# DeepNorm layer: last tile's norm sums on TensorE at the fifth K step, one normalised tile more in the first FFN block, FFN sums issued behind a later weight's split

## The chip, the cores and the metric

One core of a Trainium2 chip runs the whole kernel. The metric is the device time of one execution in microseconds. Several executions of the kernel before were timed, and one more was profiled; shares and durations come from that one.

## The reference, cut to what matters

One layer of a decoder with 256 tokens and 16 meta tokens in front (T = 272), width D = 2048, FFN width 5632, all in float32. Attention and pooling are finished where the change begins. What bears on it:

```
mix = concat(A, B) @ W_o ;  h = LN(alpha*h + mix)
z = h @ w_up                       # 2 x 5632 columns
z = causal conv of width 3 over tokens, + bias
a, g = split(z) ;  f = (gelu(a) * g) @ w_down
h = LN(alpha*h + f)
```

Both layer norms take mean and variance over the 2048 channels of a token.

## The kernel before, in words

**Tiles.** Channels lie on the 128 partitions, so h is KT = 16 tiles of 128 channels by NQ = 258 tokens (two tokens of lead for the convolution). A weight tile is 128 x 2048 float32. TensorE works on float32 in two parts: ScalarE rounds a tile to an upper part (L127, 1024 columns at a time) and VectorE subtracts it to get the lower part (L128). A product of two such tiles is three matmuls (L199 to L201). Sixteen K steps of three make one block.

**Weights.** `stream` lists all weight tiles in the order of use; `weights()` takes the next and has the tiles up to two ahead fetched and split (`prefetch`, `emit`, `fetch`), with three raw and three split buffers. A transfer starts on SP's queue when VectorE has finished with the raw buffer. `split[i]` keeps the last upper and lower instruction of tile i. `tc.issue_after(x)` makes the scheduler place what is inside behind instruction x on its engine; `behind(i)` does so for both parts of tile i. The scheduler orders each engine's queue at build time, and each engine then works in order.

**First norm.** `output(m)` makes tile m of `W_o`'s product and adds it to the residual y (L628). `about_k(m)` subtracts a rough mean (L645), squares (ScalarE, L647), and GpSimd adds tile and square into the running sums s1 and s2 (L649 to L653). It also makes `folded[m]`, tile m times the norm's scale in two parts (L656 to L660): the first blocks of the FFN start on these before the norm is known. `deviation()` sums s1 and s2 over partitions with a matmul against ones (`sum_rows`, L246, true float32), turns them with VectorE (L251), works out mean and deviation (L685 to L690, the power on GpSimd, L689) and spreads them over the rows `rs` and `m2` (L255).

**First FFN blocks.** For f < FOLDED = 4, two halves each, the block's product runs on `folded`, and `unfold` (L727 to L732) applies `rs` and `m2` afterwards. In the first of these eight blocks `deviation()` is called after K step 8. Behind each of the eight, `normalise(m)` makes normalised tiles `h_parts` (L700 and L701 on VectorE, L702 and L704 on ScalarE, L705 on VectorE): two per block. The ninth block needs all sixteen.

**FFN plan.** `ffn_plan()` interleaves one up block with one down weight of the part before. A down part is multiplied with seven products for eight (Strassen's scheme): weights of kind "A" have four products (P2, P3, P1, P5), those of kind "B" three (P7, P6, P4), each three matmuls of 512 columns (L784 to L786). Kinds A and B need subtractions on the raw weight first (L118; L122 to L124). After the last weight of a kind the products are added to the result y2: at an A end `add(c11, P2)` and `add(c12, P3)` on VectorE (L792), with copies of P1 and P5 on ScalarE (L796, L798) and accumulating transfers on GpSimd's queue (L801, L802); at a B end `add(c22, v)`, L806, L807, `add(c21, P4)`, and three transfers (L809 to L811). PSUM has four buffers for these products.

**Turning the residual.** In the blocks b = 0 to 3 behind the folded ones, VectorE turns y's 16 tiles (L855), so many per block as a tuple says; from b = 4 on `residual` moves them with transfers on ScalarE's queue (L712).

Of the kernel before, what the change touches and what calls it, by code (L numbers as in the profile page):

```python
# [14 lines left out]
ALU = mybir.AluOpType  # L15
AX = mybir.AxisListType

P = 128
# [5 lines left out]
NQ = T - Q0  # L24
KT = D // P
# [13 lines left out]
NE = NQ + 2  # L39
ALPHA = 2.0 ** 0.25  # L40
# [5 lines left out]
W = (T + 31) // 32 * 32  # L46
# [22 lines left out]
def tile_layer(ctx, tc, xt, w_first, w_proj, w_uk, w_uv, w_pool, w_o, w_up, w_down, cols, rows, rel_bias, onehot, out):  # L69
    nc = tc.nc  # L70
# [16 lines left out]
    ps = small()  # L87
# [8 lines left out]
    for item in plan:  # L96
        if item[0] == "up":
            stream.append(w_up[item[2] * FT + item[1]])
        elif item[0] == "down":
            n = PARTS[FAST]  # L100
# [5 lines left out]
    spare, last = len(stream) - PARTS[-1], len(stream) - 1  # L106
    ready, raws, split = {}, {}, {}
    state = {"next": 0, "use": 0}
# [84 lines left out]
    def product(ps, hl, m, act, lo, hi, ks=range(KT), width=P, k0=0, k1=KT):  # L193

        for n in range(k0, k1):
            k = ks[n]
            wh, wl = hl[:, 0, k * width:k * width + m], hl[:, 1, k * width:k * width + m]
            ah, al = act[k][:, 0, lo:hi], act[k][:, 1, lo:hi]
            nc.tensor.matmul(ps, wh, ah, start=n == 0, stop=False)  # L199
            nc.tensor.matmul(ps, wh, al, start=False, stop=False)  # L200
            nc.tensor.matmul(ps, wl, ah, start=False, stop=n == KT - 1)  # L201
# [6 lines left out]
    for k0, k1 in [(k, k + 1) for k in range(9)] + [(9, 12), (12, 15), (15, 16)]:  # L208
# [6 lines left out]
        if k0 % 6 == 0:  # L215
            hl = wp.tile([P, 2, 2048 + 2], F32R, tag="whl", name="whl")
# [17 lines left out]
    ones = sb.tile([P, P], F32, name="ones")  # L234
# [7 lines left out]
    def sum_rows(s):  # L242

        ps = small()
        for n, t in enumerate(s):
            nc.tensor.matmul(ps[:, :W], ones, t, start=n == 0, stop=n == len(s) - 1)  # L246
        return ps[:, :W]

    def to_partitions(r, row):

        nc.vector.transpose(r, row)  # L251
# [19 lines left out]
    ps = heads[0][0]  # L271
# [22 lines left out]
    for j in range(2):  # L294
        ps = heads[1 + j][0]
        nc.scalar.activation(ct[:, j, :], ps[:, :T], AF.Copy)
        sq = temp([P, W], "sq")
# [4 lines left out]
    ps = small()  # L302
# [66 lines left out]
    for j in range(8):  # L369
        hl = weights()  # L370
        ps = big()
# [9 lines left out]
        for i in range(2):  # L381
            r, o = slice(DI * i, DI * i + DI), slice(DI - DI * i, 2 * DI - DI * i)
# [11 lines left out]
    for h in range(H):  # L394
        ps = small()
# [18 lines left out]
    for i, (a, b) in enumerate(((0, NM), (NM, NM + P), (NM + P, T))):  # L414
# [6 lines left out]
        for g in range(2):  # L421
            ps = small()
# [33 lines left out]
    for h in range(H):  # L456
        hl = weights()
        ps = big()
# [5 lines left out]
    ps = small()  # L464
# [120 lines left out]
    for h in range(H):  # L585
        g, j = 3 - h // 2, h % 2
        if j == 0:
            df = ap_.tile([P, 2, 2, NQ], F32R, name="df", tag="df")
        hl = weights()
        ps = big()  # L590
# [49 lines left out]
    folded = []  # L640

    def about_k(m):

        yd = y[:, m, Q0:]
        nc.vector.tensor_tensor(yd, yd, acc, op=ALU.subtract)  # L645
        sq = fp.tile([P, NQ], F32, name="sq", tag="sq")
        nc.scalar.activation(s2 if m == 0 else sq, yd, AF.Square)  # L647
        if m == 1:
            nc.gpsimd.tensor_tensor(s1, y[:, 0, Q0:], yd, op=ALU.add)  # L649
        elif m > 1:  # L650
            nc.gpsimd.tensor_tensor(s1, s1, yd, op=ALU.add)
        if m:
            nc.gpsimd.tensor_tensor(s2, s2, sq, op=ALU.add)  # L653
        a = fp.tile([P, 2, NE], F32R, name="fold", tag="gp", bufs=16)
        gb = cv[:, LN1 + 2 * m:LN1 + 2 * m + 2]
        nc.scalar.activation(a[:, 0, NQ:], gb, AF.Copy)  # L656
        nc.gpsimd.tensor_tensor(a[:, 1, NQ:], gb, a[:, 0, NQ:].bitcast(F32), op=ALU.subtract)
        nc.scalar.activation(a[:, 0, :NQ], yd, AF.Copy, scale=col(LN1, 2 * m))
        nc.vector.scalar_tensor_tensor(a[:, 1, :NQ], yd, col(LN1, 2 * m), a[:, 0, :NQ].bitcast(F32), op0=ALU.mult,
                                       op1=ALU.subtract)  # L660
        folded.append(a)

    for m in range(1, KT):
        output(m)
        if m == KC - 1:
            nc.gpsimd.tensor_tensor(acc, y[:, 0, Q0:], y[:, 1, Q0:], op=ALU.add)
            for k in range(2, KC):
                nc.gpsimd.tensor_tensor(acc, acc, y[:, k, Q0:], op=ALU.add)
        if m == KC:
            ps = small()  # L670
            nc.tensor.matmul(ps[:, :NQ], ones, acc, start=True, stop=True)
            nc.scalar.activation(acc, ps[:, :NQ], AF.Copy, scale=1.0 / (KC * P))
        if m >= KC:
            while len(folded) < min(m + 1, 2 * (m - KC + 1)):
                about_k(len(folded))


    st = fp.tile([P, 4, W // 32], F32, name="st", bufs=1)
# [1 line left out]
    def deviation():  # L680
        mean, square = (of_token[:, j * NQ:j * NQ + W] for j in range(2))
        for j, r in enumerate((mean, square)):
            to_partitions(r, sum_rows([sums[:, j * NQ:j * NQ + W]]))
        mean, square = mean[:, ::32], square[:, ::32]
        nc.vector.tensor_scalar_mul(st[:, 0, :], mean, 1.0 / D)  # L685
        nc.vector.tensor_tensor(st[:, 2, :], st[:, 0, :], st[:, 0, :], op=ALU.mult)
        nc.vector.scalar_tensor_tensor(st[:, 1, :], square, 1.0 / D, st[:, 2, :], op0=ALU.mult, op1=ALU.subtract)
        nc.vector.tensor_scalar(st[:, 1, :], st[:, 1, :], 0.0, EPS, op0=ALU.max, op1=ALU.add)
        nc.gpsimd.tensor_tensor(st[:, 2, :], st[:, 1, :], half, op=ALU.pow)  # L689
        nc.vector.scalar_tensor_tensor(st[:, 3, :], st[:, 0, :], -1.0, st[:, 2, :], op0=ALU.mult, op1=ALU.mult)  # L690
        for j in range(2):
            to_row(of_token[:, j * NQ:j * NQ + W], st[:, 2 + j, :])
# [3 lines left out]
    h_parts = []  # L696
# [76 lines left out]
    def seven(kind, part, c, j):  # L773

        hl = weights()
        n = PARTS[part] // 2
        names = (("P2", 2), ("P3", 3), ("P1", 0), ("P5", 1)) if kind == "A" else (("P7", 1), ("P6", 0), ("P4", 2))
        if j == 0:
            for name, _ in names:
                held[name] = small()  # L780
        for name, w in names:
            a, i = pairs[part][j][name]
            ps, w = held[name], slice(512 * w, 512 * w + 512)
            nc.tensor.matmul(ps, a[:, 0, i], hl[:, 0, w], start=j == 0, stop=False)  # L784
            nc.tensor.matmul(ps, a[:, 0, i], hl[:, 1, w], start=False, stop=False)  # L785
            nc.tensor.matmul(ps, a[:, 1, i], hl[:, 0, w], start=False, stop=j == n - 1)  # L786
        if j < n - 1:
            return
        c11, c12, c21, c22 = (y2[:, i, w:w + 512] for i in range(2) for w in (512 * c, 1024 + 512 * c))

        def add(to, ps):
            nc.vector.scalar_tensor_tensor(to, to, 1.0 if part else ALPHA, ps, op0=ALU.mult, op1=ALU.add)  # L792

        if kind == "A":
            held["u"] = fp.tile([P, 512], F32, name="u", tag="u1", bufs=1, padded_shape=[P, NQ + W])
            nc.scalar.activation(held["u"], held["P1"], AF.Copy)  # L796
            held["v"] = fp.tile([P, 512], F32, name="v", tag="u2", bufs=1, padded_shape=[P, NQ + W])
            nc.scalar.activation(held["v"], held["P5"], AF.Copy)  # L798
            add(c11, held["P2"])
            add(c12, held["P3"])  # L800
            nc.gpsimd.dma_start(c11, held["u"], accum_op=ALU.add)  # L801
            nc.gpsimd.dma_start(c12, held["v"], accum_op=ALU.add)  # L802
        else:
            u, v = held["u"], held["v"]
            add(c22, v)
            nc.vector.tensor_tensor(u, u, held["P6"], op=ALU.add)  # L806
            nc.vector.tensor_tensor(v, u, held["P7"], op=ALU.add)  # L807
            add(c21, held["P4"])
            nc.gpsimd.dma_start(c12, u, accum_op=ALU.add)  # L809
            nc.gpsimd.dma_start(c21, v, accum_op=ALU.add)  # L810
            nc.gpsimd.dma_start(c22, v, accum_op=ALU.add)  # L811
# [4 lines left out]
    for item in plan:  # L816
# [34 lines left out]
        b = 2 * (f - FOLDED) + half_  # L851
        upper, lower = split[state["use"] + 1]
        with tc.issue_after(lower):
            for m in turns[:(2, 4, 5, 5)[b] if 0 <= b < 4 else 0]:
                nc.vector.transpose(y[:, m, NM:], y[:, m, NM:])  # L855
                turns.remove(m)
        with tc.issue_after(upper):
# [7 lines left out]
        if f < FOLDED:  # L865
            k = 0
            if f + half_ == 0:
                product(ps[:, :NE], hl, P, folded, 0, NE, k1=8)
                deviation()
                k = 8  # L870
            product(ps[:, :NE], hl, P, folded, 0, NE, k0=k)
            with behind(state["use"]):
                while len(h_parts) < min(KT, 2 * (2 * f + half_ + 1)):
                    normalise(len(h_parts))
            both.append(ps)
            if half_ == 0:
                continue
            both = [conv(i * FT + f, i, unfold(both[i]), pair[:, f % 2]) for i in range(2)]
        else:
            product(ps[:, :NQ], hl, P, h_parts, 0, NQ)  # L880
            both.append(conv(half_ * FT + f, half_, ps, pair[:, f % 2]))
            if half_ == 0:
                continue
# [197 lines left out]
```

## Time and profile before

| | |
|---|---|
| three runs, median | 1045.23 us (1044.82 to 1045.94) |
| profiled execution | 1045.81 us |
| its span, first to last instruction | 1044.0 us |
| granted TensorE clock, mean | 0.997 |
| up and down transfers | 88 and 80, each 1024 KB |

The profile's engines are PE (TensorE matmuls), PEld (its weight loads), DVE (VectorE), ACT (ScalarE), POOL (GpSimd) and SP (transfer queue). A row of a group reads: line, engine, operation, output<-input, shape, count. A row of the order in time begins with the start and the duration in us; a bracket at its end gives the engine's idle time before it and what ended that. A row of the waits reads: who waited, for whom, total us, times, longest. Matmuls overlap, so their durations are longer than the distance between their starts.

### The profile page before, as it was taken

The numbers are of one execution on the slowest core, as the hardware profiler recorded it, in microseconds if no ns is written. First come the engines' busy times: TensorE is split into PE (matmuls) and PEld (weight loads), VectorE is DVE, ScalarE is ACT, GpSimd is POOL, SyncE is SP. The second block draws the span as 40 slices with busy tenths as digits, with TensorE's granted clock in tenths as the row PEclk, the third lists the DMA queues.
The fourth block names the chain that finished last, engine by engine and source line by source line (L and its number), as shares of the span: only waits on it lengthen the run. The fifth ranks groups of instructions, "written<-read, shape, count | busy, mean of one in ns | idle before, by whom it ended". The sixth has DMA issues, their size and how long they took to land.

```text
span 1044.0 us, 19202 instructions
## 1 busy us (share of the span) xinstructions
PE 1034.6 (99%) x7639; PEld 984.2 (94%) x7639; DVE 888.2 (85%) x1401; ACT 623.2 (60%) x1000; POOL 194.8 (19%) x248
## 2 busy tenths in 40 slices
PE   9999999999999999999999999999999999999997
PEld 8999999999999999989999999999999999999986
DVE  6879568758779997799989989899898999999876
ACT  6666446645448855456565655656555666555665
POOL 1200014125340021211112111120111201220031
PEclk9999999999999999999999999999999999999998
DMA  8755643454554578789887787877878878787865
GB/s 319 256 180 216 226 145 117 146 189 164 180 196 149 175 223 238 235 291 298 278 285 274 262 291 267 287 273 269 281 268 287 275 277 278 268 286 270 292 214 159
DMA packets 59754, 250.28 MB, mean 240 GB/s; under 512 B 21734, under 2 KB 22416, under 8 KB 32656
## 3 DMA queue, kind: packets, MB, share of 16 engines
q1 hardware_dynamic: 34592, 230.42, 61.1%
q0 software_dynamic: 7888, 16.14, 8.2%
q10 hardware_dynamic: 17184, 2.49, 1.5%
q8 instruction: 60, 0.98, 0.4%
q14 instruction: 30, 0.25, 0.1%
HBM read 232.50 MB, written 2.11 MB: 225 GB/s over the span
## 4 chain that ended last, share of the span: by engine, by line
PE 85%; DVE 6%; issue 3%; DMA 3%; ACT 2%; POOL 1%; SPq 0%; POOLq 0%; DVEq 0%; ACTq 0%
PE mm L200 21%; PE mm L199 21%; PE mm L201 21%; PE at L785 5%; PE at L784 5%; PE at L786 5%; DVE whl L128 3%; DMA wraw<-in_w_first 1%; DMA wraw<-in_w_down 1%; ACT whl L127 1%; DMA wraw<-in_w_up 1%; DVE hp L705 0%; DVE x L700 0%; DVE x L701 0%; PE at L358 0%
## 5 line engine op out<-in xcount | busy, mean ns | idle before, releaser
L128 DVE TENSOR_TENSOR whl<-wraw,whl 128x1024 fp32r<-128x1024 f32 (+1 forms) x416 | 488.5, 1208 | 39.5 <-ACT whl L127 38.7
L127 ACT ACTIVATE whl<-wraw 128x1024 fp32r<-128x1024 f32 (+1 forms) x416 | 402.9, 1015 | 115.5 <-issue 27.1
L200 PE MATMUL mm<-hp,whl 128*128 128x258 f32 x1280 | 362.4, 283 | 0.7 <-DVE hp L705 0.7
L199 PE MATMUL mm<-hp,whl 128*128 128x258 f32 x1280 | 361.4, 282 | 0.0
L201 PE MATMUL mm<-hp,whl 128*128 128x258 f32 x1280 | 361.2, 282 | 0.0
L200 PEld LDWEIGHTS mm<-hp,whl 128*128 128x128 f32 x1280 | 242.7, 190 | 4.0 <-DVE hp L705 0.9
L199 PEld LDWEIGHTS mm<-hp,whl 128*128 128x128 f32 x1280 | 242.5, 189 | 3.2
L201 PEld LDWEIGHTS mm<-hp,whl 128*128 128x128 f32 x1280 | 242.9, 190 | 0.1
L199 PE MATMUL mm<-xp,whl 128*128 128x256 f32 (+5 forms) x384 | 111.9, 291 | 0.0
L200 PE MATMUL mm<-xp,whl 128*128 128x256 f32 (+5 forms) x384 | 108.7, 283 | 0.0
L201 PE MATMUL mm<-xp,whl 128*128 128x256 f32 (+5 forms) x384 | 108.7, 283 | 0.0
L719 ACT ACTIVATE z<-mm,cv 128x256 f32<-128x256 f32 x40 | 22.5, 563 | 95.6 <-PE mm L201 95.6
L199 PEld LDWEIGHTS mm<-xp,whl 128*128 128x128 f32 x384 | 72.4, 189 | 1.0 <-issue 0.5
L200 PEld LDWEIGHTS mm<-xp,whl 128*128 128x128 f32 x384 | 72.3, 188 | 0.4
L201 PEld LDWEIGHTS mm<-xp,whl 128*128 128x128 f32 x384 | 72.4, 188 | 0.3 <-DVE whl L128 0.2
L785 PE MATMUL at<-whl,gp 128*128 128x512 f32 x180 | 71.2, 396 | 0.8 <-DVE whl L128 0.8
L786 PE MATMUL at<-whl,gp 128*128 128x512 f32 x180 | 71.0, 395 | 0.0
L784 PE MATMUL at<-whl,gp 128*128 128x512 f32 x180 | 69.4, 395 | 0.0
L719 ACT ACTIVATE za<-mm,cv 128x256 f32<-128x256 f32 x40 | 22.5, 562 | 70.9 <-PE mm L201 66.2
L759 POOL TENSOR_TENSOR forms<-za 128x128 f32<-128x128 f32 x20 | 23.3, 1167 | 203.5 <-DVE za L737 203.5
L756 POOL TENSOR_TENSOR forms<-za 128x128 f32<-128x128 f32 x20 | 21.2, 1059 | 203.5 <-DVE za L737 139.1
L786 PEld LDWEIGHTS at<-whl,gp 128*128 128x128 f32 x180 | 33.8, 188 | 7.8
(346 smaller groups left out, 1925.4 us busy)
## 6 DMA issues: line engine op xcount, KB each, us to landing
wraw<-in_w_up SPq DMA_DIRECT2D x88, 1024.0 KB, 5.0
wraw<-in_w_down SPq DMA_DIRECT2D x80, 1024.0 KB, 6.8
wraw<-in_w_proj SPq DMA_DIRECT2D x24, 1024.0 KB, 5.0
wraw<-in_w_o SPq DMA_DIRECT2D x16, 1024.0 KB, 4.9
y<-v POOLq DMA_DIRECT2D x27, 256.0 KB, 8.5
y<-u POOLq DMA_DIRECT2D x18, 256.0 KB, 4.7
wraw<-in_w_first SPq DMA_DIRECT2D x8, 304.0 KB, 5.5
x<-in_xt SPq DMA_DIRECT2D x1, 2176.0 KB, 8.9
```

Of the source, the lines that this page charges most:

```text
L127: upper = nc.scalar.activation(hl[:, 0, c], raw[:, c], AF.Copy)
L128: lower = nc.vector.tensor_tensor(hl[:, 1, c], raw[:, c], hl[:, 0, c].bitcast(F32), op=ALU.subtract)
L199: nc.tensor.matmul(ps, wh, ah, start=n == 0, stop=False)
L200: nc.tensor.matmul(ps, wh, al, start=False, stop=False)
L201: nc.tensor.matmul(ps, wl, ah, start=False, stop=n == KT - 1)
L719: nc.scalar.activation(z, src[:, 2:NQ], AF.Identity, bias=col(C_B, j), scale=col(C_W, 3 * j + 2))
L756: nc.gpsimd.tensor_tensor(s[:, 0], a21, a22, op=ALU.add)
L759: nc.gpsimd.tensor_tensor(s[:, 3], a11, a21, op=ALU.subtract)
L784: nc.tensor.matmul(ps, a[:, 0, i], hl[:, 0, w], start=j == 0, stop=False)
L785: nc.tensor.matmul(ps, a[:, 0, i], hl[:, 1, w], start=False, stop=False)
L786: nc.tensor.matmul(ps, a[:, 1, i], hl[:, 0, w], start=False, stop=j == n - 1)
```

## The change

Last tile's sums: `about_k` leaves out GpSimd's additions for tile 15 and returns that tile and its square; `sum_rows` adds both on TensorE to the same PSUM sums (the tile has 258 columns, the sums have 288). `deviation()` is called after K step 5 instead of 8. One tile more: the first block is followed by three normalised tiles instead of two, so each later count is one higher, until the eighth block has one left. Later split: each `add` of the FFN is issued behind the lower split of the weight two ahead of the one in use. The tuple of turned tiles is (0, 5, 5, 6) instead of (2, 4, 5, 5).

```diff
-            nc.tensor.matmul(ps[:, :W], ones, t, start=n == 0, stop=n == len(s) - 1)
+            nc.tensor.matmul(ps[:, :t.shape[1]], ones, t, start=n == 0, stop=n == len(s) - 1)
...
-        elif m > 1:
+        elif 1 < m < KT - 1:
             nc.gpsimd.tensor_tensor(s1, s1, yd, op=ALU.add)
-        if m:
+        if 0 < m < KT - 1:
             nc.gpsimd.tensor_tensor(s2, s2, sq, op=ALU.add)
...
         folded.append(a)
+        return yd, sq
...
-                about_k(len(folded))
+                last_two = about_k(len(folded))
...
-            to_partitions(r, sum_rows([sums[:, j * NQ:j * NQ + W]]))
+            to_partitions(r, sum_rows([sums[:, j * NQ:j * NQ + W], last_two[j]]))
...
         def add(to, ps):
-            nc.vector.scalar_tensor_tensor(to, to, 1.0 if part else ALPHA, ps, op0=ALU.mult, op1=ALU.add)
+
+            with tc.issue_after(split[min(state["use"] + 1, last - 1)][1]):
+                nc.vector.scalar_tensor_tensor(to, to, 1.0 if part else ALPHA, ps, op0=ALU.mult, op1=ALU.add)
...
-            for m in turns[:(2, 4, 5, 5)[b] if 0 <= b < 4 else 0]:
+            for m in turns[:(0, 5, 5, 6)[b] if 0 <= b < 4 else 0]:
...
-                product(ps[:, :NE], hl, P, folded, 0, NE, k1=8)
+                product(ps[:, :NE], hl, P, folded, 0, NE, k1=5)
                 deviation()
-                k = 8
+                k = 5
...
-                while len(h_parts) < min(KT, 2 * (2 * f + half_ + 1)):
+                while len(h_parts) < min(KT, 2 * (2 * f + half_ + 1) + 1):
```

## The prediction

> **What bounds the kernel now.** I read the page's first part, then TensorE's waits, then the order in time around each wait. First the busy times, and the four waits that bear on the change or on the end.
>
> ```profile
> PE 1034.6 (99%) x7639; PEld 984.2 (94%) x7639; DVE 888.2 (85%) x1401; ACT 623.2 (60%) x1000; POOL 194.8 (19%) x248
> ...
> PE at L972 <- ACT diag L970: 1.5, 1, 1.5
> ...
> PE at L785 <- DVE whl L128: 0.8, 1, 0.8
> PE mm L200 <- DVE hp L705: 0.7, 1, 0.7
> PE at L246 <- POOL sums L653: 0.5, 1, 0.5
> ```
>
> TensorE is busy 99% of the span. Nothing done beside it is worth time unless it ends a wait of TensorE, and the three last waits, 2.0 us together, are all that the three edits can aim at. The wait at L972 is in the tail, which no edit touches. So the question is small on both sides: what these three cost in full, what the change adds on TensorE, and whether a moved instruction makes a new wait. The waits' own figures are too small, since TensorE also loses time in starting again; I take the loss from start to start instead.
>
> The stretch around the norm sums, all engines in order of time:
>
> ```profile
> 303.38 0.28 PE L199 MATMUL mm<-fold,whl 128*128 128x260 f32 x1
> ...
> 304.05 0.43 DVE L645 TENSOR_TENSOR x<-x,acc 128x258 f32<-128x258 f32 x1
> ...
> 304.60 0.41 ACT L647 ACTIVATE sq<-x 128x258 f32<-128x258 f32 x1
> 304.62 0.64 POOL L651 TENSOR_TENSOR sums<-sums,x 128x258 f32<-128x258 f32 x1 [3.52 <-DVE x L645]
> ...
> 304.73 1.61 DVE L128 TENSOR_TENSOR whl<-wraw,whl 128x1024 fp32r<-128x1024 f32 x1 [0.26 <-ACT whl L127]
> ...
> 305.18 0.28 PE L199 MATMUL mm<-fold,whl 128*128 128x260 f32 x1
> ...
> 305.22 1.63 POOL L653 TENSOR_TENSOR sums<-sums,sq 128x258 f32<-128x258 f32 x1
> ...
> 305.31 1.05 ACT L127 ACTIVATE whl<-wraw 128x1024 fp32r<-128x1024 f32 x1
> ...
> 306.15 0.28 PE L201 MATMUL mm<-fold,whl 128*128 128x260 f32 x1
> ...
> 306.26 0.87 DVE L659 SCALAR_TENSOR_TENSOR fold<-x,cv,fold 128x258 fp32r<-128x258 f32 x1
> ...
> 306.90 1.24 PE L246 MATMUL at<-sums,ones 128*128 128x288 f32 x4 [0.47 <-POOL sums L653]
> 307.05 1.21 DVE L128 TENSOR_TENSOR whl<-wraw,whl 128x1024 fp32r<-128x1024 f32 x1
> ...
> 308.09 0.28 PE L200 MATMUL mm<-fold,whl 128*128 128x260 f32 x1
> 308.19 1.06 DVE L251 STREAM_TRANSPOSE of_token<-at 128x288 f32<-128x288 f32 x2
> ```
>
> From 303.38 to 305.18 TensorE starts 15 matmuls, 0.12 us each, so a K step of three takes 0.36. After the eighth step (306.15) it should go on at 306.27 and does at 306.90: 0.63 lost. From 306.15 to 308.09 are 1.94 us; less two normal starts (0.24) and the wait, the two sums themselves take 1.07 us (four records, two to a product).
>
> The first block that reads the normalised tiles, where the second wait is, and its releaser on VectorE:
>
> ```profile
> 356.17 0.28 PE L199 MATMUL mm<-hp,whl 128*128 128x258 f32 x1
> 357.11 0.39 PE L200 MATMUL mm<-hp,whl 128*128 128x258 f32 x1 [0.67 <-DVE hp L705]
> 357.34 0.28 PE L201 MATMUL mm<-hp,whl 128*128 128x258 f32 x1
> ...
> 357.71 0.28 PE L201 MATMUL mm<-hp,whl 128*128 128x258 f32 x1
> ```
>
> ```profile
> 314.50 1.22 DVE L128 TENSOR_TENSOR whl<-wraw,whl 128x1024 fp32r<-128x1024 f32 x1
> ...
> 356.63 0.76 DVE L705 TENSOR_TENSOR hp<-x,hp 128x258 fp32r<-128x258 f32 x2
> ```
>
> Two starts in 1.17 us where 0.24 would do: 0.93 lost on the low part of tile 14. Tile 15's comes 0.34 after it and is just in time. The engine behind this is VectorE, without a gap for 45 us:
>
> ```profile
> 312.00:357.00 45.00, 44.44 (x371) 44.24 (x370) 44.94 (x103) 37.16 (x65) 0.00 (x0) 1.00 0.47 160
> ```
>
> (The columns are length, then busy time of PE, PEld, DVE, ACT, POOL.) The third wait is in a "B" weight of the first down part; below it the VectorE rows 30 us earlier, and three links from the chain of work that ended last:
>
> ```profile
> 453.89 0.39 PE L784 MATMUL at<-whl,right 128*128 128x512 f32 x1
> ...
> 455.53 0.50 PE L784 MATMUL at<-whl,gp 128*128 128x512 f32 x1
> 456.87 0.50 PE L785 MATMUL at<-whl,gp 128*128 128x512 f32 x1 [0.84 <-DVE whl L128]
> ...
> 457.43 0.28 PE L199 MATMUL mm<-hp,whl 128*128 128x258 f32 x1
> ```
>
> ```profile
> 427.70 0.69 DVE L122 TENSOR_TENSOR wraw<-wraw 128x512 f32<-128x512 f32 x1
> 432.30 0.69 DVE L792 SCALAR_TENSOR_TENSOR y<-y,at 128x512 f32<-128x512 f32 x1 [3.92 <-PE at L786]
> 432.90 0.68 DVE L123 TENSOR_TENSOR wraw<-wraw 128x512 f32<-128x512 f32 x1
> ...
> 436.15 4.90 DVE L128 TENSOR_TENSOR whl<-wraw,whl 128x1024 fp32r<-128x1024 f32 x4
> ```
>
> ```profile
> 446.99 6.80 DMA wraw<-in_w_up
> 453.89 1.07 ACT whl L127
> 454.99 1.84 DVE whl L128 x2
> ```
>
> And a steady "A" tile, with the VectorE splits in front of it:
>
> ```profile
> 536.65 0.39 PE L784 MATMUL at<-whl,gp 128*128 128x512 f32 x1
> ...
> 539.21 0.40 PE L786 MATMUL at<-whl,gp 128*128 128x512 f32 x1
> ```
>
> ```profile
> 534.96 2.35 DVE L128 TENSOR_TENSOR whl<-wraw,whl 128x1024 fp32r<-128x1024 f32 x2
> ```
>
> In steady state 12 matmuls start 0.233 us apart (11 intervals in 2.56). The nine of the late B tile should take 2.10 and take 3.54 (453.89 to 457.43): 1.44 lost. The cause lies far back. At the first A end VectorE took the wait for PSUM (L792) ahead of two weight subtractions (L123, L124), stood 3.92 us, freed its raw buffers late, and the w_up transfer started only at 446.99.
>
> **The change part by part.**
>
> *Sums.* TensorE now adds tile 15 itself, at K step 5, where the next start is 305.18. Its inputs: tile 14's sums are long done (the pause of 3.52 in L651's row), the tile is ready at 304.48, its square at 305.01. So no wait is left: −0.63. Added are two products of 258 columns. At the rate of the 288-column ones they cost 1.07 × 258/288 = 0.96; without the restart inside the 1.07 about 0.86. I take 0.90 (bounds 0.86 and 0.96). TensorE leaves this place 0.27 us **later** than before.
>
> What is earned here is earned on VectorE. GpSimd's two additions for tile 15 go. Beside them L128 took 1.61 instead of 1.21, and L659 0.87; a VectorE operation of this size starts the next after some 0.4 (L645 takes 0.43). In the new order the sequence on VectorE up to the transposes is unchanged. Laid out with undisturbed lengths: L128 304.73 to 305.87, L659 to 306.27, the second L128 when ScalarE's upper half is there (305.31 + 1.05 = 306.36), so about 306.39, and the transposes 1.14 later at 307.53 instead of 308.19: 0.66 earlier. Both sums are in PSUM by then (305.18 + 1.97 for eight records, and the matmul's 0.28). Bounds: 0, if the long rows have another cause, to 0.66, where ScalarE stops it.
>
> The Trainium skill, "SBUF — State Buffer", section "SBUF: two separate sides", calls the ports that VectorE and GpSimd share an exclusive lock: whichever starts first has it for its whole instruction, against VectorE operations with two SBUF inputs too. The rows look like it (L128 ends as if started when L651 ended). By that rule the full 0.66 comes; if the rows were something else, none.
>
> *One tile more in the first block.* Between the first L700 and tile 15's L705 both builds have the same 91 or so VectorE instructions (16 each of L700, L701, L705, 15 of L128, the unfold and conv steps); only their order differs. So tile 15 is not earlier by this edit itself, but tile 14 is: it now comes with tile 13, a weight split and the unfold steps before tile 15. Laying the new order end to end with the rows' lengths, I find two short waits for ScalarE, about 0.1 each, so tile 15's copy is ready 0.44 earlier than 357.39: 356.95, and TensorE can start on it at 357.01 (it started 0.06 behind the copy at 357.11). TensorE reaches this matmul at 356.17 + 0.48 + 0.27 = 356.92. What remains is 0.1 of waiting and 0.11 of restart: the following matmul starts at 357.24 instead of 357.71. **Sums and tile together: −0.47.** Bounds: with the VectorE chain no earlier the same matmul starts at 357.68 (−0.03); with no wait at all at 357.02 (−0.69). The weight splits that move back behind the third tile (the first from 314.50 to about 316.7) serve the fourth block. It starts at 303.38 + 1.70 for the sums + 3 × 5.76 = 322.4, so TensorE doesn't see them.
>
> *Adds behind a later split.* At the first A end VectorE no longer stands 3.92 us: L123 and L124 run first, and both adds come after the B weight's split, when P2 and P3 are complete. Following the new order (subtractions to 429.5, conv to 431.5, splits and adds to 434.7, the next two splits to 436.9), VectorE is some 4 us ahead of the 441.05 at which the same four splits ended before, every raw buffer and so each transfer on SP's queue too. TensorE's late half was 1.34 us late. Against 4 us the wait goes: −1.44, and I keep 0 as the other end. Behind the waiting adds on VectorE now stand the next up block's splits; P2's PSUM buffer is freed up to 3 us later, but the next user starts an up block (5.76 us) after the A end. At each B end the add of c22, formerly early, joins the cluster: 0.60 us more (432.30 to 432.90) ahead of a split that ended 537.31 and whose weight TensorE takes up at 539.44. Cost nothing, cover 2.1 us. GpSimd's accumulating DMAs follow the adds; their targets are not read for tens of us.
>
> *Transposes 0, 5, 5, 6.* The same 16, none in the first block: 0.7 us less for VectorE just where tile 15 was late, one more in the fourth. The residual's transfers on ScalarE's queue come after all of them in both. Nothing on TensorE.
>
> **Sum.** 0.47 + 1.44 = 1.91 us. The profiled execution took 1045.81 (span 1044.0), which gives 1043.9; the runs' median is 0.58 lower, 1045.23, and gives **1043.3**.
>
> **The rivals.**
>
> *The VectorE chain is not shortened* (the long rows come from elsewhere, or ScalarE's waits eat it): 0.03 + 1.44 = 1.47, 1043.8. For it: my layout leaves only 0.44. Against: an L128 without GpSimd beside it, 2.3 us later, takes 1.21.
>
> *The late B half stays*, because the w_up transfer, 6.80 us, is stretched by traffic and not by its start: only 0.47 is gained, 1044.8. Against: the 3.92 row.
>
> *Everything goes*: 0.69 + 1.44 = 2.13, 1043.1, the most that the waits allow.
>
> *A new wait at the B ends.* c22's 0.60 delays the up weight's split at nine B ends. It decides once VectorE is over 2.1 us later than in the row at 534.96; then each end costs up to 0.60 and a restart of 0.11, nine of them 6.4, less 1.9: 1049.7, slower. For it: VectorE is 85% busy and the cluster grows to four operations. Against: the cover is three times the delay, and the early add's 0.60 is saved before.
>
> **How the numbers follow.** Forecast (both waits go, chain about half shortened) 0.57; chain not shortened 0.13; late half stays 0.10; everything goes 0.13; new wait 0.07. About 0.2% is what a measurement of this kernel can tell from no change, here 2.09 us, or 1043.14. The forecast lies 0.2 us above that bound, with runs spread over 1.1 us: I give 45 in 100 of it to faster, and 75 in 100 of "everything goes": 0.26 + 0.10 + 0.01 from the rest = 0.37. Slower is the new wait, 0.07; same is the remainder, 0.56. The range takes in all but the new wait and the runs' tails: 1042.5 to 1044.9.
>
> **What would show it.** Right: no TensorE wait at L246, eight records there and GpSimd absent; L128 near 304.7 at 1.2 us, the transposes near 307.5; at most 0.1 us on L705's low parts; no stop on VectorE at the first A end and no wait at L785. Wrong: a wait of TensorE on L128 behind a B end, on x or sq at L246, or a transpose start still near 308.2.

## The result and the profile after

| | before | after | ratio (95% interval) |
|---|---|---|---|
| first comparison, 14 runs each | 1046.13 us (1044.82 to 1047.37) | 1043.73 us (1042.91 to 1044.88) | 0.9978 (0.9970 to 0.9986) |
| again, beside experiments, 27 and 11 runs | 1045.41 us (1044.40 to 1047.47) | 1043.34 us (1042.97 to 1045.31) | 0.9982 (0.9974 to 0.9991) |
| span of the profiled execution | 1044.0 us | 1041.3 us | |
| granted clock in it | 0.997 | 0.998 | |

The changed kernel is faster by 0.22%, 2.4 us (1.5 to 3.1 by the interval's ends). The forecast was 1043.3.

The busy times on the page of the changed kernel:

```profile
PE 1033.3 (99%) x7643; PEld 984.3 (95%) x7643; DVE 891.0 (86%) x1401; ACT 621.0 (60%) x1000; POOL 189.5 (18%) x246
```

Its list of TensorE's waits (who, for whom, total us, times, longest):

```profile
PE at L975 <- ACT diag L973: 1.5, 1, 1.5
PE at L89 <- POOL warm L86: 1.1, 1, 1.1
PE mm L992 <- DVE whl L191: 0.2, 1, 0.2
```

The waits on the norm sums, on tile 14 and in the late B half (the second 1024 columns of the first B weight, which came late) are gone, and a wait on the row sums of the last weight, in the tail, is new. The stretch around the norm sums, in order of time (rows of VectorE and TensorE):

```profile
303.59 1.23 DVE L128 TENSOR_TENSOR whl<-wraw,whl 128x1024 fp32r<-128x1024 f32 x1 [0.26 <-ACT whl L127]
...
303.92 0.28 PE L201 MATMUL mm<-fold,whl 128*128 128x260 f32 x1
...
304.04 0.65 PE L246 MATMUL at<-sums,ones 128*128 128x288 f32 x2
...
304.73 0.48 DVE L659 SCALAR_TENSOR_TENSOR fold<-x,cv,fold 128x258 fp32r<-128x258 f32 x1
...
306.00 0.28 PE L200 MATMUL mm<-fold,whl 128*128 128x260 f32 x1
...
306.39 1.06 DVE L251 STREAM_TRANSPOSE of_token<-at 128x288 f32<-128x288 f32 x2
```

The first fold matmul started at 302.24 here and at 303.38 before. Against that start the transposes come after 4.15 us, where it was 308.19 - 303.38 = 4.81. From the fifth step's last matmul (303.92) to the sixth step's second (306.00) are 2.08 us; less two normal starts (0.24) the four products take 1.84.

Tiles 14 and 15 in the first block that reads them, in order of time:

```profile
354.23 1.21 DVE L128 TENSOR_TENSOR whl<-wraw,whl 128x1024 fp32r<-128x1024 f32 x1
...
355.36 0.42 DVE L706 TENSOR_TENSOR hp<-x,hp 128x258 fp32r<-128x258 f32 x1
...
355.50 0.28 PE L199 MATMUL mm<-hp,whl 128*128 128x258 f32 x1
...
355.83 0.19 PEld L200 LDWEIGHTS mm<-hp,whl 128*128 128x128 f32 x1 [0.26 <-DVE hp L706]
355.83 0.39 PE L200 MATMUL mm<-hp,whl 128*128 128x258 f32 x1
...
356.06 0.28 PE L201 MATMUL mm<-hp,whl 128*128 128x258 f32 x1
```

TensorE's list of waits has nothing here, since the bracket stands at the weight load and not at the matmul. But the start after 355.50 should be at 355.62 and is at 355.83: 0.21 of waiting. The next one, at 356.06, is another 0.11 late: starting again. Only tile 15 is late, and a weight split stands on VectorE right ahead of its last step.

VectorE at the first A end, and at the end of the rows the start of the transfer that was late before (SPq, the transfer queue):

```profile
426.05 0.69 DVE L122 TENSOR_TENSOR wraw<-wraw 128x512 f32<-128x512 f32 x1
426.77 0.69 DVE L123 TENSOR_TENSOR wraw<-wraw 128x512 f32<-128x512 f32 x1
427.50 0.69 DVE L124 TENSOR_TENSOR wraw<-wraw 128x512 f32<-128x512 f32 x1
...
432.26 1.27 DVE L795 SCALAR_TENSOR_TENSOR y<-y,at 128x512 f32<-128x512 f32 x2
433.46 2.35 DVE L128 TENSOR_TENSOR whl<-wraw,whl 128x1024 fp32r<-128x1024 f32 x2
...
441.75 0.33 SPq L112 DMA_DIRECT2D wraw<-in_w_up  x1
```

The stop of 3.92 us is gone; the same splits end at 435.81, before at 441.05. Counted from the first fold matmul that is 133.57 and 137.67, so 4.1 us earlier, and the transfer starts 4.1 us earlier too (139.51 and 143.61). And the new wait in the tail:

```profile
1019.01 0.28 PE L991 MATMUL mm<-whl,gp 128*128 128x258 f32 x1
1019.28 0.15 DVE L191 TENSOR_TENSOR whl<-total,whl 128x2 fp32r<-128x2 f32 x1
...
1019.49 0.39 PE L992 MATMUL mm<-whl,gp 128*128 128x258 f32 x1 [0.20 <-DVE whl L191]
...
1019.72 0.28 PE L993 MATMUL mm<-whl,gp 128*128 128x258 f32 x1
```

From 1019.01 to 1019.72 two starts take 0.71 where 0.24 would do.

**Four stretches.** Outside four stretches the traces agree to 0.1 us, apart from the start and from the end behind the tail, which takes 8.79 and 9.27 us in the two traces of one kernel ("after, c22 early, no tile") and 8.91 to 9.00 in the others. They are, from start to start on TensorE: the sums (first fold matmul to first matmul on a normalised tile), the tiles (from there to the first FFN matmul), the B weight (its first FFN matmul to the next weight's) and the tail (first down matmul to the tail's last matmul, L990 before and L993 after). All traces of this study but one ("c22's cost made large", below, where the tail is in another order), in us, worked out from the order in time; the names are those of the experiments:

```
kernel                          sums   tiles   B weight   tail    all four
before                         47.77   52.81     9.28    44.77    154.63
before, again                  47.78   52.82     9.07    44.71    154.38
after                          47.88   52.20     7.82    45.20    153.10
after, again                   47.88   52.19     7.82    44.97    152.86
sums only                      47.89   51.87    10.17    45.44    155.37
sums only, again               47.88   51.88     8.60    45.75    154.11
one tile more only             47.77   53.03     9.02    44.71    154.53
later adds only                47.78   52.82     7.83    45.59    154.02 
after, c22 early               47.88   52.20     7.83    44.71    152.62
after, c22 early, no tile      47.89   51.88     7.83    44.72    152.32
the same, again                47.88   51.88     7.83    45.04    152.63
after, GpSimd's adds kept      47.88   52.86     7.82    45.66    154.22
after, sums at K step 8        47.89   51.88     7.82    44.99    152.58
```

After against before, the four give 1.53 us in the first pair of traces and 1.52 in the second. The spans differ by 2.7 in the first pair, because the kernel before had reached its first fold matmul 1.14 us later, over instructions that are the same in both; in the second pair it reached it 0.31 earlier (303.06 and 303.37).

### The profile page after: what moved, and what is told of

The parts are those of the page before. It is cut to its first block, busy times and chain, and to the rows that moved or that the text cites. A ratio compares the mean times of both kernels' runs of the same rounds, so it can differ in the third digit from the quotient of the medians.

```text
span 1041.3 us, 19198 instructions
## 1 busy us (share of the span) xinstructions
PE 1033.3 (99%) x7643; PEld 984.3 (95%) x7643; DVE 891.0 (86%) x1401; ACT 621.0 (60%) x1000; POOL 189.5 (18%) x246
## 4 chain that ended last, share of the span: by engine, by line
PE 89%; DVE 5%; issue 3%; ACT 1%; POOL 1%; DMA 1%; POOLq 0%; DVEq 0%; ACTq 0%
PE mm L200 22%; PE mm L199 22%; PE mm L201 22%; PE at L786 6%; PE at L785 6%; PE at L787 6%; DVE whl L128 2%; DMA wraw<-in_w_down 1%; PE mm L268 1%; PE mm L269 1%; PE mm L270 1%; ACT whl L127 1%; DVE x L701 0%; DVE hp L706 0%; PE at L358 0%
## 5 line engine op out<-in xcount | busy, mean ns | idle before, releaser
L128 DVE TENSOR_TENSOR whl<-wraw,whl 128x1024 fp32r<-128x1024 f32 (+1 forms) x416 | 486.3, 1203 | 37.7 <-ACT whl L127 36.8
```

What stands on the lines that cost most here:

```text
L128: lower = nc.vector.tensor_tensor(hl[:, 1, c], raw[:, c], hl[:, 0, c].bitcast(F32), op=ALU.subtract)
```

## The experiments

The diffs shown are against the changed kernel; "one tile more alone" and "the later adds alone" are the kernel before with that part of the change's diff and nothing else. Line numbers differ by up to four between the kernels. The experiments up to "After without the tile edit" ran on one chip, where the kernel before took 1045.25 us (33 runs); only the second trace of the sums alone comes from another.

**The sums alone** (adds, tiles and tuple as before):

```diff
-            with tc.issue_after(split[min(state["use"] + 1, last - 1)][1]):
-                nc.vector.scalar_tensor_tensor(to, to, 1.0 if part else ALPHA, ps, op0=ALU.mult, op1=ALU.add)
+            nc.vector.scalar_tensor_tensor(to, to, 1.0 if part else ALPHA, ps, op0=ALU.mult, op1=ALU.add)
...
-                while len(h_parts) < min(KT, 2 * (2 * f + half_ + 1) + 1):
+                while len(h_parts) < min(KT, 2 * (2 * f + half_ + 1)):
```

> Only the sums edit (tile 15's sums on TensorE, after K step 5); two normalised tiles in the first block, the adds and the turned tiles as before. Theory (the sums cost TensorE 0.27 us and bring VectorE's transposes forward by 0.66 us, which alone ends the wait at the ninth block): eight records at the sums without a wait, no wait of TensorE on hp, so 0.93 - 0.27 = 0.66 us gained up to the ninth block's end; the late B half of 1.44 us is still there. Time 0.7 us below before. Rival (the wait on hp goes only because of the third tile in the first block): a wait on hp's low part of 0.3 us or more remains and nothing or 0.27 us is lost.

1044.67 us, ratio 0.9998 (0.9989 to 1.0007): no difference that the runs can show. The profiled execution took longest of the eleven (1045.85; seven took 1044.03 to 1044.87), and the table tells where its time went. The sums cost 0.12 and the tiles gain 0.94, 0.82 net, without any wait on tiles 14 and 15. VectorE there, in order of time:

```profile
352.80 0.76 DVE L702 TENSOR_TENSOR x<-x,of_token 128x258 f32<-128x258 f32 x2
...
354.69 0.77 DVE L706 TENSOR_TENSOR hp<-x,hp 128x258 fp32r<-128x258 f32 x2 [0.33 <-ACT hp L705]
...
356.44 1.23 DVE L128 TENSOR_TENSOR whl<-wraw,whl 128x1024 fp32r<-128x1024 f32 x1 [0.52 <-ACT whl L127]
```

Both tiles come as a pair, ahead of the weight split: from the first fold matmul on, 16 splits of weights stand ahead of tile 15's last step, and 17 in the kernel before and in the changed one. But in this execution the B weight cost 0.89 more than before and the tail 0.67 more, and ate the gain.

**The sums alone, a second trace:**

> The sums on TensorE alone, a second trace. In its first one the 0.83 us gained up to the first down part were gone again behind it: the late B half of the first up weight cost 2.34 us instead of 1.45, because its transfer took 7.69 us instead of 6.80, and the tail took 45.44 us instead of 44.77. Theory A: the transfers land when the traffic of all the queues lets them, so what TensorE gains ahead of them is given back there; the late half costs 2.2 to 2.4 us again. Theory B: the transfer's length jitters from run to run; the late half costs anything from 1.2 to 2.4 us, and with 1.2 to 1.5 the kernel is 0.8 us faster than the kernel before up to the down parts.

One run, 1044.76 us. The B weight lost 8.60 - 7.83 = 0.77, in the first trace 2.34. So theory B, by two traces: the same kernel's transfer, started 142.79 us behind the first fold matmul in both, differs in length from one execution to the next. (They ran on two chips; what the chip has of it isn't known.) The transfer in the chain of work that ended last, of the first trace:

```profile
445.46 7.69 DMA wraw<-in_w_up
```

And of the second:

```profile
445.70 6.12 DMA wraw<-in_w_up
```

**One tile more alone:**

> Only the tile edit (three normalised tiles behind the first block), the rest as before. Theory (the work on VectorE ahead of tile 15 is the same, only ordered otherwise): tile 14 is in time, tile 15's low part comes where it came before, so the wait moves from tile 14 to tile 15 and the block ends at most 0.1 us earlier; the waits at the sums (0.63 us lost) and at the late B half (1.44) remain. Time within 0.2 us of before. Rival (the tile edit itself ends the wait): no wait on hp, 0.9 us gained.

1045.97 us, ratio 1.0009 (1.0000 to 1.0018): 0.7 above before, where at most 0.2 was expected. The profiled execution was the shortest of the eleven (1045.14), so its trace can't show all of that. In it the tiles lose 0.22 more than before. Tile 15 is what is late now (TensorE in order of time):

```profile
356.39 0.39 PE L199 MATMUL mm<-hp,whl 128*128 128x258 f32 x1 [0.24 <-ACT hp L704]
357.16 0.39 PE L200 MATMUL mm<-hp,whl 128*128 128x258 f32 x1 [0.38 <-DVE hp L705]
```

**The later adds alone:**

> Only the adds of the FFN behind the later split; sums, tiles and turned tiles as before. Theory: VectorE doesn't stop for 3.9 us at the first A end, the late B half is gone (-1.44 us), the waits at the sums and on hp remain, and in the tail TensorE loses some 0.2 to 0.5 us on the last weight's row sums, because c22's add delays the last raw buffer: time 1.0 to 1.4 us below before. Rival (the late half goes because VectorE is earlier after the first norm or by the turned tiles): the B half is still late by over 0.5 us and the time that of before.

1044.48 us, ratio 0.9993 (0.9985 to 1.0002). The B weight gains 1.45, and the tail loses 0.82, more than the 0.2 to 0.5 expected. TensorE stops there twice, on the last weight's split (0.28 lost) and on its row sums (0.59 lost); the larger stop in the list of waits:

```profile
PE mm L991 <- DVE whl L191: 0.3, 1, 0.3
```

**After without the tile edit, c22's add early.** c22 is added from v, which is complete long before; here its addition is taken out of the later place again:

```diff
-            add(c22, v)
+            nc.vector.scalar_tensor_tensor(c22, c22, 1.0 if part else ALPHA, v, op0=ALU.mult, op1=ALU.add)
...
-                while len(h_parts) < min(KT, 2 * (2 * f + half_ + 1) + 1):
+                while len(h_parts) < min(KT, 2 * (2 * f + half_ + 1)):
```

> The change without its tile edit (two normalised tiles behind the first block), and with the add of c22 free to go early as before; the other adds stay behind the later split. Theory: sums -0.66 with no wait on hp, late B half -1.44, no wait in the tail: 2.1 us below before, the best so far. Rival (the third tile is what ends the wait on hp, and c22's place is nothing): a wait on hp of 0.3 us or more and a tail wait of 0.4 us as after the change, 1.5 us below before or less.

1043.28 us, ratio 0.9983 (0.9974 to 0.9992). TensorE has no wait from the first fold matmul to the one on diag at the end, and takes 2.31 us less in the four stretches than in the first trace of before. (This trace is of the longest of the eleven, 1044.51: its first fold matmul came at 304.52, later than in any other trace.)

**The next three** and the second trace of the sums alone ran on another chip (before: 1045.41 us). The first is the diff above without its second part:

> The changed kernel with one line undone: c22's addition goes back to its early place, ahead of the B end's cluster of additions; all else is kept. Theory: its 0.60 us in the last cluster frees the last raw buffer 0.6 us later, so the last w_down transfer and the last row sums come later, and TensorE stands in the tail. Then from the first down matmul to the last matmul of the tail it should be 44.7 us again, as in the kernel before without a wait (the changed kernel took 45.20), with no wait of TensorE on the row sums, and the median should be 0.4 to 0.5 us under that of the changed kernel. The pause of 0.33 us at tile 15's low part stays. Rival: the tail's wait comes from the length of the last transfers, which differs by some tenths from run to run (9.06 to 9.47 us in five traces); then a wait of 0.3 to 0.9 us is there in this kernel too, and the median is that of the changed kernel.

1043.37 us, ratio 0.9980 (0.9971 to 0.9989).

> The changed kernel with c22's addition early and without the edit that normalises one tile more in the first block; the same kernel as in the first set, here beside the others on one chip. Theory: with the sums on TensorE the last two tiles come as a pair ahead of a weight split, and TensorE doesn't wait on them; with one tile more in the first block tile 15 is alone in the last block and its last step stands behind a weight split of 1.21 us, which costs 0.33 us. So this should be 0.3 us faster than the kernel with c22 early alone and 0.7 to 0.8 us faster than the changed kernel, and have no wait between the first fold matmul and the last down matmul. Rival: the edit costs nothing that a median shows, and this kernel and the one with c22 early alone are equal.

1043.35 us, ratio 0.9981 (0.9972 to 0.9989).

> The changed kernel once more, as the control for the two others, and for a second trace. Both theories: about 2.4 us under the kernel before. By the first (c22's addition causes the tail's wait) the tail takes 45.1 to 45.6 us again from the first down matmul to the last; by the rival (the transfers' own jitter) it can as well take 44.7 with no wait. The pause at tile 15's low part should be 0.33 us and the VectorE weight split beside the fold tile 1.23 us in both.

1043.34 us, in the result's table. The three medians are equal, so neither of the two expected gains, 0.4 to 0.5 and 0.7 to 0.8, shows in a median. In the traces the tile edit's 0.32 is there each time (52.20 and 52.19 with it, 51.88 without). The tail is 44.71 with c22 early, as the theory has it, but without the tile edit it is 45.04 in this trace, with c22 just as early. To see why, take three times behind the first down matmul: the end of the last-but-one pair of splits on VectorE, which frees raw buffers, ScalarE's start on the last weight, and the end. In the changed kernel, in order of time (TensorE, VectorE, ScalarE, TensorE):

```profile
987.17 0.40 PE L837 MATMUL mm<-whl,gp 128*128 128x512 f32 x1
...
997.13 2.35 DVE L128 TENSOR_TENSOR whl<-wraw,whl 128x1024 fp32r<-128x1024 f32 x2
...
1008.87 2.01 ACT L127 ACTIVATE whl<-wraw 128x1024 fp32r<-128x1024 f32 x2 [0.42 <-DMA wraw<-in_w_down]
...
1032.37 0.28 PE L993 MATMUL at<-whl,gp 128*128 128x256 f32 x1
```

And in the one with c22 early:

```profile
987.82 0.40 PE L837 MATMUL mm<-whl,gp 128*128 128x512 f32 x1
...
997.17 2.35 DVE L128 TENSOR_TENSOR whl<-wraw,whl 128x1024 fp32r<-128x1024 f32 x2
...
1007.52 2.01 ACT L127 ACTIVATE whl<-wraw 128x1024 fp32r<-128x1024 f32 x2 [0.44 <-DMA wraw<-in_w_down]
...
1032.53 0.28 PE L993 MATMUL at<-whl,gp 128*128 128x256 f32 x1
```

The splits end 12.31 and 11.70 us behind the first down matmul, the last weight is taken up after 21.70 and 19.70, the tail is 45.20 and 44.71. The same for all:

```
                        splits end   last weight   tail over 44.71
c22's add in the cluster
  after                    12.31        21.70          0.49
  after, again             12.31        21.47          0.26
  later adds only          12.31        22.08          0.88
  GpSimd's adds kept       12.31        22.16          0.95
  sums at K step 8         12.31        21.49          0.28
c22's add early
  before                   11.71        21.28          0.06
  before, again            11.70        20.56          0.00
  sums only                11.70        21.94          0.73
  sums only, again         11.71        22.26          1.04
  one tile more only       11.70        21.14          0.00
  c22 early                11.70        19.70          0.00
  c22 early, no tile       11.71        20.08          0.01
  the same, again          11.70        21.53          0.33
```

The tail's loss is the time by which the last weight comes later than 21.2 us, to 0.01 or 0.02 in each row. And c22's addition delays the splits by 0.60 each time. The last transfer starts 12.52 or 12.53 us behind the first down matmul in all of the first group and after 11.92 to 12.41 in the second, so 0.1 to 0.6 of the delay reaches its start. The time at which the last weight is taken up spreads over 0.7 us in the first group and 2.6 in the second. The groups' means are 21.78 and 21.06, so the delay may well pass through, but the spread is larger than it.

**c22's cost made large:**

```diff
             add(c22, v)
+            if (kind, part, c) == [x[:3] for x in plan if x[0] == "B"][-1]:
+                for _ in range(5):
+                    with tc.issue_after(split[min(state["use"] + 1, last - 1)][1]):
+                        nc.vector.scalar_tensor_tensor(c22, v, 0.0, c22, op0=ALU.mult, op1=ALU.add)
```

> The changed kernel with five more VectorE operations like c22's addition, which change nothing (c22 + 0 times v), in the last B end alone, ahead of the last weight splits: 3.0 us more before the split that frees the last raw buffer, where c22's own late addition is 0.6. Theory (the last w_down transfer starts when that split is done, and the row sums in the tail wait for it): ScalarE begins with the last weight 24.0 to 25.5 us behind the first down matmul, instead of 21.5 and 21.7 in the two traces of the changed kernel, and from the first down matmul to the last of the tail it takes 47 to 48.5 us instead of 45.0 and 45.2. Rival (the landing is set by the traffic of the queues, which in nine traces put it at 19.7 to 22.3 us with either place of c22's addition): it stays within 22.5, and the tail takes at most 45.7 us.

One run, 1045.08 us. The splits end 15.32 behind the first down matmul, 3.01 later, and the last weight is taken up after 22.85, 1.15 and 1.38 later than in the two traces of the changed kernel. That is neither of the two: part of the delay goes through, the rest is made good by a faster landing (the last transfer took 7.23 us, in the two traces of the changed kernel 9.10 and 8.86). The tail's stretch stayed at 44.71, because the scheduler also put TensorE's products on the row sums in another place; the loss came behind it instead, in the wait on diag, 1.5 in the changed kernel's list of waits and here:

```profile
PE at L979 <- ACT diag L977: 2.8, 1, 2.8
```

So how much c22's later place costs in the tail stays open, between nothing and 0.6 us.

**GpSimd's additions kept.** GpSimd adds tile 15 once more, into a part of y2 that is overwritten before anything reads it (y2 is allocated earlier for this); TensorE's sums stay:

```diff
-        elif 1 < m < KT - 1:
-            nc.gpsimd.tensor_tensor(s1, s1, yd, op=ALU.add)
-        if 0 < m < KT - 1:
-            nc.gpsimd.tensor_tensor(s2, s2, sq, op=ALU.add)
+        elif m > 1:
+            nc.gpsimd.tensor_tensor(s1 if m < KT - 1 else y2[:, 0, :NQ], s1, yd, op=ALU.add)
+        if m:
+            nc.gpsimd.tensor_tensor(s2 if m < KT - 1 else y2[:, 1, :NQ], s2, sq, op=ALU.add)
```

> The changed kernel, in which GpSimd still makes its two additions for tile 15, into space that nothing reads; TensorE's sums, their place and all else are kept. So only the neighbour of VectorE's operations comes back. Theory (VectorE shares a way to the data with GpSimd and waits for it): the weight split beside the fold tile takes 1.6 us again instead of 1.23 and the fold tile's second half 0.87 instead of 0.48, the first of the transposes starts 4.8 us behind the first fold matmul instead of 4.15, and everything on VectorE up to tile 15 is 0.66 later, so that TensorE's pause at tile 15's low part grows from 0.2 us of lost time to about 0.9. Rival (the long rows have another cause): 1.23, 0.48, 4.15 and 0.2 as in the changed kernel.

One run, 1044.78 us. VectorE in order of time; the first fold matmul is at 302.82:

```profile
304.17 1.61 DVE L128 TENSOR_TENSOR whl<-wraw,whl 128x1024 fp32r<-128x1024 f32 x1 [0.26 <-ACT whl L127]
305.70 0.86 DVE L660 SCALAR_TENSOR_TENSOR fold<-x,cv,fold 128x258 fp32r<-128x258 f32 x1
306.48 1.21 DVE L128 TENSOR_TENSOR whl<-wraw,whl 128x1024 fp32r<-128x1024 f32 x1
307.62 1.06 DVE L251 STREAM_TRANSPOSE of_token<-at 128x288 f32<-128x288 f32 x2
```

GpSimd in the same stretch:

```profile
304.05 0.64 POOL L652 TENSOR_TENSOR y<-sums,x 128x258 f32<-128x258 f32 x1 [3.52 <-DVE x L646]
304.65 1.62 POOL L654 TENSOR_TENSOR y<-sums,sq 128x258 f32<-128x258 f32 x1
```

The transposes are at 4.80 again, and the tiles' stretch is 0.66 longer than in the changed kernel: 52.86 against 52.20. The rows fit into each other like one queue: L128 takes its usual 1.1 us counted from the end of L652 (304.69), L654, an operation of 0.6 us, ends 0.5 behind L128 (305.78), and L660 ends 0.3 behind L654 (306.27).

**The sums at K step 8:**

```diff
-                product(ps[:, :NE], hl, P, folded, 0, NE, k1=5)
+                product(ps[:, :NE], hl, P, folded, 0, NE, k1=8)
                 deviation()
-                k = 5
+                k = 8
```

> The changed kernel with the norm sums at the eighth K step as in the kernel before, and not at the fifth. Theory (the place counts): TensorE reaches the sums 1.08 us later, the second pair of products is complete only about 0.3 us behind the time at which VectorE is free, so the second transpose comes 0.2 to 0.5 us later; and the weight split goes back among the first normalised tiles, ahead of the third. The loss at tiles 14 and 15 is then 0.3 to 0.9 us instead of 0.2. Rival (the place is free as long as TensorE makes the sums): 0.2 us as in the changed kernel.

One run, 1043.48 us. The theory was wrong: with the sums three steps later TensorE has no pause at tiles 14 and 15 at all (51.88). VectorE took the first transpose at the same 4.15 us (307.25 - 303.10), filled the time to the second with statistics, and came to tile 15's last step 0.31 us sooner (VectorE in order of time):

```profile
307.25 0.48 DVE L251 STREAM_TRANSPOSE of_token<-at 128x288 f32<-128x288 f32 x1
307.76 0.17 DVE L686 TENSOR_SCALAR st<-of_token 128x9 f32<-128x9 f32 x1
...
308.05 0.48 DVE L251 STREAM_TRANSPOSE of_token<-at 128x288 f32<-128x288 f32 x1
...
354.78 1.22 DVE L128 TENSOR_TENSOR whl<-wraw,whl 128x1024 fp32r<-128x1024 f32 x1
355.91 0.42 DVE L706 TENSOR_TENSOR hp<-x,hp 128x258 fp32r<-128x258 f32 x1
```

(355.91 - 303.10 = 52.81 behind the first fold matmul; after: 355.36 - 302.24 = 53.12.) The same 17 weight splits stand ahead of it, in another order, and VectorE loses 0.3 us less on the way. Where, was not taken apart.

**The kernel before, a second trace:**

> The kernel before, a second trace, to tell what of its waits is of the program and what of the single run. Theory: the waits on the norm sums and on tile 14 are of the program and come again with 0.63 and 0.82 us of lost time; the late B half and the tail hang on a transfer and can come out anywhere from 0.7 to 2.3 us and from 0 to 0.9 us. Rival: all four come out as in the first trace, the late half at 1.4 to 1.5 us and the tail at 0.1.

One run, 1045.23 us. The theory held: 0.63 at the sums and 0.82 at tile 14 came again to the hundredth, the B weight lost 1.24 instead of 1.45, the tail nothing. The transfer in its chain of work:

```profile
446.69 6.58 DMA wraw<-in_w_up
```

## Why the prediction was right, and where it was not

The time and the main mechanism were right: three waits go, most of their worth with them. Step by step:

- **Sums: 0.27 later on TensorE.** 0.11 to 0.14. The stretch of the products grew by 0.77 (1.84 - 1.07), not by 0.90. The restart of some 0.1 that the old 1.07 held goes with the wait; the prediction took it out of the price of the added products, but not out of the old ones.
- **VectorE 0.66 earlier at the transposes.** 0.66, and the trace with GpSimd's kept additions, where it is gone, shows that it comes from their absence. The Trainium skill, "SBUF — State Buffer", section "SBUF: two separate sides", calls the shared ports an exclusive lock, held for a whole instruction; the rows of that trace agree, in both directions: each engine's operation ends as if it had started its work when the other's ended.
- **Sums and tile together: -0.47.** -0.50. Tile 15's copy was ready 53.54 us behind the first fold matmul, 0.47 earlier than before (54.01), where 0.44 was laid out; the wait left on it was 0.21, not 0.1, since TensorE came sooner. But the tile edit has no part in the gain. The sums alone give -0.82 and no wait; the tile edit **costs** 0.32 of it. The step that failed is the one that took tile 14's earlier place for a help and left tile 15 behind a weight split; without the tile edit the pair is ready after 52.79 us, ahead of that split.
- **Adds: -1.44.** -1.46 in the first pair of traces. The late half is gone with the adds alone as well, and all nine traces with later adds have none, while all five without have one, of 0.77, 1.19, 1.24, 1.45 and 2.34 us. That VectorE's stop causes it was right; that it costs 1.44 was one execution's number, since the transfer takes 6.12 to 7.69 us.
- **c22's 0.60 at the B ends: nothing, cover 2.1 us.** Right at the B ends before the last: from the weight behind the late B weight to the first down matmul all fourteen traces take the same 527.1 us. Not right at the last one, where the next weights are down weights and the last raw buffer is freed behind the cluster: there the last weight came between 1.5 us ahead of and 1.0 us behind the 21.2 at which TensorE needs it, so no cover can be counted on. With it failed "the tail, which no edit touches". The tail lost 0.43 and 0.26 us in the two pairs. What c22 has of that is open, as said above; the rest is the transfer's own spread.
- **Transposes 0, 5, 5, 6: nothing.** No wait near them in any trace. The tuple wasn't changed alone, but the sums alone, with the old one, and "after, c22 early, no tile", with the new one, have the same 47.88 and 51.88 us in the first two stretches.
- **Sum 1.91.** 1.53 and 1.52 by the traces. The medians give 2.4 and 2.1, with intervals that reach down to 1.5 and 0.9; 1.5 lies in both, and the 0.6 to 0.9 between them isn't accounted for by any trace. That the time came out within 0.4 us of 1043.3 is in part luck: the traces give 0.4 less than the sum, and the kernel before measured 1046.13 in the comparison where the forecast had started from 1045.23.

Of the rivals, "the VectorE chain is not shortened" and "the late half stays" are refuted. "Everything goes" was more than happened: one pause of 0.32 stayed and a wait in the tail came. "A new wait at the B ends" named the right operation with the wrong place, and its price there is at most 0.6 us once, not nine times.

## What to carry to other kernels

Lay out the engine that feeds the waits with and without each edit, not only with all of them: by the traces, one of three edits here took back 0.32 of the 0.82 us that another had earned, and their sum hid it. Move an operation past a buffer's release only after looking at the last use of that place, where the following work is different and the cover is another. And take a wait on a transfer from several executions before it is priced.

## What was not expected of the hardware

- The same 1024 KB transfer behind the same stop landed after 6.12, 6.50, 6.58, 6.80 and 7.69 us in five traces. In the tail the last weight could be taken up 19.7 to 22.3 us behind the first down matmul.
- A delay of 3.0 us ahead of the last transfers came out as 1.15 to 1.38 us when the last weight was taken up.
- TensorE loses some 0.11 us when it starts again after a pause, on top of the wait that the list shows (355.83 to 356.06 and 1019.49 to 1019.72, 0.23 instead of 0.12); and the pause of the changed kernel at tile 15 (355.50 to 355.83) isn't in TensorE's list at all, since there the weight load waited, and not the matmul.
